# Attention's transposes and value products, taken for two groups of keys at a time

## The chip, the core and the metric

The kernel is one program on 1 core of one Trainium2 chip. The metric is the device time of one execution in microseconds (us). Three executions of the kernel before gave 2945.81, 2949.18 and 2950.16; their median is 2949.18.

## The reference, cut to what matters

One layer of a hybrid decoder on a sequence of 2048 tokens and 1024 channels, all in float32: a normalized input, one input projection, two kinds of causal attention with 8 heads of 64 channels each, an output projection, and a gated MLP with a short convolution. The change lies in the attention. Per head, with queries in blocks of 128:

```python
# forgetting attention ("fox")
s = jnp.einsum('bhqd,bhkd->bhqk', q_blk, k) * scale + F_blk[..., None] - F[:, :, None, :]
p = jax.nn.softmax(jnp.where(causal, s, -jnp.inf), axis=-1)
out = jnp.einsum('bhqk,bhkd->bhqd', p, v)
# stick-breaking attention ("sb")
log_one_minus_beta = jnp.where(strict, jax.nn.log_sigmoid(-z), 0.0)
rest = lax.cumsum(log_one_minus_beta, axis=3, reverse=True) - log_one_minus_beta
a = jnp.where(strict, jnp.exp(jax.nn.log_sigmoid(z) + rest), 0.0)
out = jnp.einsum('bhqk,bhkd->bhqd', a, v)
```

## The kernel before, in words

**Precision.** TensorE (PE) multiplies float32 operands in a rounded form (float32r). To keep accuracy an operand is stored as a high part (the rounded copy, made on ScalarE, ACT) and a low part (the value minus its high part, mostly made on VectorE, DVE), and a product becomes two or three matmuls.

**Order of the work.** Until about 1515 us the program runs 32 attention units: 4 head pairs times 4 blocks of 512 tokens, first of kind sb, then of kind fox. While `attend` goes through a unit, `interleave` steps other generators between its yields: the projections of later units (`proj`, lines 342 and 413 on PE), late conditioning work, and in the last two units the first output projection (line 912). The generators only give the order in which the program is traced. The framework's scheduler then sets the order on each engine, by its own estimate of when each instruction's inputs are ready. On the chip each engine takes its own queue in that order, and an instruction that waits holds up all behind it on its engine. `tc.issue_after(x)` puts what its block traces on the engine of `x` behind `x` in that engine's queue; it makes nothing wait for the end of `x`, and what the block traces on another engine is left as it is.

**A unit.** `attend` takes two pairs of query blocks and two heads. For each such head, `logits` (lines 596 and 597) multiplies queries by up to 512 keys into a PSUM bank of the tag qk (2 banks). In sb, ACT takes two sigmoids (630 and 631), GpSimd (POOL) masks (633), and DVE runs a scan from right to left (636) that leaves the weights of 128 queries in a tile `a`; keys are taken in chunks of 512 from the last to the first. In fox, DVE adds the forget sums (675) and ACT takes the exponential of the whole row (679), which leaves the weights in a tile `p`.

**A group.** `weighted` (600 to 618) takes 2 key tiles of 128 and 2 query blocks of 128: four transposes on PE (606) into a PSUM bank of the tag pt (3 banks), ordered (key 1, query 0), (key 0, query 0), (key 0, query 1), (key 1, query 1); on the diagonal the first of these is left out. ACT copies the bank to the high half of a tile `at` (610; `at` has 3 buffers), DVE writes the low half (611), and four value products (615) with `at` as the moving operand add to one PSUM bank `o` of the tag pv (1 bank; in the second-last unit the tag bc): per key tile first high, then low. A fox head with 2j + 2 key tiles has j + 1 groups, an sb chunk has one or two. After the head ACT and DVE read `o` (737, 738).

In all there are 576 groups with 2176 transposes and 2304 value products.

Of the kernel before, what the change touches and what calls it, by code (L numbers as in the profile page):

```python
# [12 lines left out]
AF = mybir.ActivationFunctionType  # L13
# [4 lines left out]
P = 128  # L18
# [16 lines left out]
def kernel(ctx: ExitStack, tc: tile.TileContext, x, c, w_ada, b_ada, g_attn, w_in, b_fgate,  # L35
                      g_out_fox, g_out_sb, w_out, g_mlp, w_up, conv_w, conv_b, w_down, g_final, out):
    nc = tc.nc
# [3 lines left out]
    def f(t):  # L41
        return t.bitcast(F32)
# [31 lines left out]
    ident = edge[:, TB - P:TB]  # L74
# [128 lines left out]
    last = {}  # L203
# [13 lines left out]
    b = pv()  # L217
# [6 lines left out]
    for r, src in ((R_GA, g_attn), (R_GM, g_mlp), (R_GF, g_out_fox), (R_GS, g_out_sb), (R_BA, b_ada)):  # L224
        n = src.shape[1] // P
# [368 lines left out]
    def logits(cw, qcols, hl, Q, K):  # L594
        b = qk()
        nc.tensor.matmul(b[:, :cw], Q[:, hl, 0, qcols], K[:, hl, :cw], start=True, stop=False)  # L596
        marks.append(nc.tensor.matmul(b[:, :cw], Q[:, hl, 1, qcols], K[:, hl, :cw], start=False, stop=True).ins)  # L597
        return b

    def weighted(o, kts, blk, V, hl, first, last, diag):  # L600
        b = pt()
        at = sb.tile([P, 2, 2 * 2 * P], F32R, name="at", tag="at", bufs=3)
        order = [(1, 0), (0, 0), (0, 1), (1, 1)]
        for i, (kk, qi) in enumerate(order):
            if not (diag and i == 0):
                nc.tensor.transpose(b[:, i * P:(i + 1) * P], blk(kts[kk], qi), ident)  # L606
        lo = P if diag else 0
        if diag:
            nc.scalar.activation(at[:, :, 0:P], edge[:, 0:2 * P].rearrange("p (a n) -> p a n", n=P), AF.Copy)
        copies = [nc.scalar.activation(at[:, 0, lo:], b[:, lo:], AF.Copy).ins,  # L610
                  nc.vector.tensor_sub(at[:, 1, lo:], b[:, lo:], f(at[:, 0, lo:])).ins]  # L611
        for kk, kt in enumerate(kts):
            for w in range(2):
                rhs = at[:, w].rearrange("p (s q) -> p s q", q=P)[:, 0:4:3, :] if kk else at[:, w, P:3 * P]
                m = nc.tensor.matmul(o[:, 0:2 * P], V[kt // 4][:, kt % 4, hl, :], rhs,  # L615
                                     start=first and kk == 0 and w == 0, stop=last and kk == 1 and w == 1)
        sums.append(m.ins)
        step[:] = [m.ins] + copies

    def sb_head(j, qc, hl, Q, K, V, o):  # L620
        n = (2 * j + 2 + 3) // 4
        right = [None, None]
        for ch in range(n - 1, -1, -1):
            at = []
            for qi in range(2):
                need = min(512, (2 * j + qi + 1) * P - ch * 512)
                b = logits(max(need, 2 * P), slice((qc + qi) * P, (qc + qi + 1) * P), hl, Q, K[ch])
                r = sx.tile([P, 512], F32, name="r", bufs=7)
                a = sx.tile([P, 512], F32, name="a", bufs=7)
                nc.scalar.activation(r[:, :need], b[:, :need], AF.Sigmoid)  # L630
                nc.scalar.activation(a[:, :need], b[:, :need], AF.Sigmoid, scale=-1.0)  # L631
                if right[qi] is None:
                    nc.gpsimd.affine_select(out=a[:, need - P:need], in_=a[:, need - P:need], pattern=[[-1, P]],
                                            base=-1, channel_multiplier=1, compare_op=ALU.is_ge, fill=0.0)
                rev = a[:, 0:need][:, ::-1]
                nc.vector.tensor_tensor_scan(rev, r[:, 0:need][:, ::-1], rev,  # L636
                                             0.0 if right[qi] is None else right[qi][:, 0:1], ALU.mult, ALU.add)
                right[qi] = a
                at.append(a)
            yield  # L640
            nk = min(4, 2 * j + 2 - 4 * ch)
            for m in range(0, nk, 2):
                kts = [4 * ch + m, 4 * ch + m + 1]
                weighted(o, kts, lambda kt, qi: at[qi][:, (kt - 4 * ch) * P:(kt - 4 * ch + 1) * P], V, hl,
                         ch == n - 1 and m == 0, ch == 0 and m == nk - 2, kts[0] == 2 * j)
                yield

    def load_sums(p):
        sums = [[], []]
# [7 lines left out]
    def fox_head(j, qc, hl, Q, K, V, o, Fb, ls):  # L657
        n = (2 * j + 2 + 3) // 4
        rows_ = []
        for qi in range(2):  # L660
            W = (2 * j + qi + 1) * P
            a = sx.tile([P, S], F32, name="p", bufs=4)
            mn = None
            for ch in range(n):
                need = min(512, W - ch * 512)
                b = logits(max(need, 2 * P), slice((qc + qi) * P, (qc + qi + 1) * P), hl, Q, K[ch])
                sl = slice(ch * 512, ch * 512 + need)
                m2 = sx.tile([P, 1], F32, name="mn", bufs=8)
                add = Fb[ch]
                if ch == n - 1:  # L670
                    add = px.tile([P, TB], F32, name="Fd", tag="hf_a", bufs=2)
                    mask[:] = [nc.gpsimd.affine_select(
                        out=add[:, :need], in_=Fb[ch][:, :need], pattern=[[-1, need]], base=need - P,
                        channel_multiplier=1, compare_op=ALU.is_ge, fill=BIG).ins]
                nc.vector.tensor_tensor_reduce(out=a[:, sl], in0=b[:, :need], in1=add[:, :need], scale=1.0,  # L675
                                               scalar=3e38 if mn is None else mn, op0=ALU.add, op1=ALU.min,
                                               accum_out=m2)
                mn = m2
            nc.scalar.activation(a[:, 0:W], a[:, 0:W], AF.Exp, scale=-1.0, bias=mn, accum_out=ls[:, hl, qc + qi:qc + qi + 1])  # L679
            rows_.append(a)  # L680
            yield
        for m in range(0, 2 * j + 2, 2):
            weighted(o, [m, m + 1], lambda kt, qi: rows_[qi][:, kt * P:(kt + 1) * P], V, hl, m == 0, m == 2 * j,
                     m == 2 * j)
            yield

    sums, step, mask = [], [], []
    deferred = []
# [137 lines left out]
    def attend_steps(u):  # L826
        kind, p, tb = u
        if kind == "fox":
            return sum(2 * (2 + 2 * tb + j2 + 1) for j2 in range(2)) + 1
        return sum(2 * (tb + 1 + 2 * tb + j2 + 1) for j2 in range(2)) + 1  # L830
# [199 lines left out]
    for i, u in enumerate(units):  # L1030
# [10 lines left out]
        n = attend_steps(u)  # L1041
# [212 lines left out]
    first = {"raw": [], "ws": []}  # L1254
# [41 lines left out]
    for u in range(1, NU):  # L1296
        for c in range(8 if u == 1 else 0, 16):
            t, n, q = chunk(u, c)
# [8 lines left out]
    def bank_a():  # L1307
        return bank(psd, "o", 4)
# [138 lines left out]
    for sblk, order in enumerate(orders):  # L1447
        after = None
        if sblk == 0:
# [5 lines left out]
            after = finish_last  # L1455
# [39 lines left out]
        a, b = bank_a(), bank_a()  # L1495
# [189 lines left out]
    for i in range(7):  # L1685
        nxt = {}
        kept = []
        for s in range(2):
# [4 lines left out]
            if left:  # L1693
                half, n = lefts[i]
                ops = left_over(s, half)
            for kp in range(NKP):
# [5 lines left out]
                w = bops[kp]  # L1702
# [60 lines left out]
```

## Time and profile before

| what | us |
| --- | --- |
| median of three executions | 2949.18 |
| lowest, highest | 2945.81, 2950.16 |
| span of the profiled execution, first to last instruction | 2941.4 |
| PE busy in it | 2867.8 |
| DVE, ACT, POOL busy | 2179.5, 1686.0, 901.1 |

The page gives the span alone for the profiled execution; the median of the timed ones is 7.8 us above that span, which is what lies around it. PE is an engine with two rows: PE is the matmul, PEld the load of the stationary operand, which goes beside the matmul before it. The trace models the end of a matmul, so its duration holds time in which the next one already streams; what a matmul costs is read from where a row of equal matmuls ends and the row after it ends.

### The profile page before, as it was taken

What the parts mean: (1) busy time and instruction counts of PE and PEld (TensorE: products, weight loads), DVE (VectorE), ACT (ScalarE), POOL (GpSimd) and SP (SyncE); (2) the same over time, 40 slices, a digit from 0 to 9 for tenths busy, and PEclk for the clock granted to TensorE, in tenths of its full rate; (3) what the DMA queues carried; (4) which work ended last, traced back from release to release, by engine and by line L of the source; (5) the groups of instructions that cost most, each with busy time, mean ns of one, the idle gap of its engine ahead of it and who ended that gap; (6) DMA issues with size and microseconds to landing.
All of it is one profiled execution on the core that took longest, in us unless ns stands there. A gap on an engine that the chain in (4) does not pass through costs nothing.

```text
span 2941.4 us, 45922 instructions
## 1 busy us (share of the span) xinstructions
PE 2867.8 (97%) x15772; PEld 2459.7 (84%) x15772; DVE 2179.5 (74%) x3464; ACT 1686.0 (57%) x3187; POOL 901.1 (31%) x967
## 2 busy tenths in 40 slices
PE   8999999999999999999999999999999999999998
PEld 7888888888988988888888788888788888888887
DVE  5787778877886656658843788888998888575476
ACT  5776767677776656658744554444444445433342
POOL 0431322243032423231213344444254543142200
PEclk8999999999999999999999999999999999999999
DMA  9749756867469794794537775554754444975644
GB/s 293 255 139 321 236 188 207 301 211 229 162 212 356 269 277 139 232 323 140 182 120 233 245 232 128 130 136 129 236 132 125 130 130 132 309 257 185 216 158 151
DMA packets 348346, 601.89 MB, mean 205 GB/s; under 512 B 34672, under 2 KB 178800, under 8 KB 348112
## 3 DMA queue, kind: packets, MB, share of 16 engines
q1 hardware_dynamic: 324208, 558.06, 57.7%
q0 software_dynamic: 10880, 20.97, 4.3%
q10 hardware_dynamic: 13024, 19.93, 1.9%
q8 instruction: 124, 2.03, 0.3%
q14 instruction: 110, 0.90, 0.1%
HBM read 420.77 MB, written 177.02 MB: 203 GB/s over the span
## 4 chain that ended last, share of the span: by engine, by line
PE 46%; DMA 3%; DVE 2%; SPq 1%; ACT 1%; issue 1%; POOL 0%; DVEq 0%; ACTq 0%; POOLq 0%
PE ps_o L1315 19%; PE ps_t L1315 7%; PE ps_o L1614 6%; PE ps_t L1614 3%; PE ps_bc L1614 3%; PE ps_o L912 1%; PE ps_pv L615 1%; DMA r<-rstd 1%; PE ps_bc L912 1%; PE ps_pt L606 1%; PE ps_o L1609 1%; DMA wo<-wos 1%; DMA hm<-hf_m 1%; SPq L895 1%; DVE op L46 1%
## 5 line engine op out<-in xcount | busy, mean ns | idle before, releaser
L1315 PE MATMUL ps_o<-op,wu 128*128 128x512 f32 x2592 | 608.0, 389 | 2.0 <-DVE snap L1366 1.5
L1315 PEld LDWEIGHTS ps_o<-op,wu 128*128 128x128 f32 x2592 | 486.2, 188 | 103.9 <-DVE snap L1366 1.9
L611 DVE TENSOR_TENSOR at<-ps_pt,at 128x512 fp32r<-128x512 f32 (+1 forms) x576 | 366.1, 652 | 100.2 <-ACT at L610 97.3
L636 DVE TENSOR_TENSOR_SCAN a<-r,a 128x512 f32<-128x512 f32 (+2 forms) x320 | 368.3, 1167 | 77.8 <-ACT a L631 39.9
L342 PE MATMUL ps_pj<-hp,w_qk 128*128 128x512 f32 x1512 | 411.2, 403 | 14.5 <-DMA hp<-hs 12.9
L610 ACT ACTIVATE at<-ps_pt 128x512 fp32r<-128x512 f32 (+1 forms) x576 | 318.5, 576 | 139.1 <-PE ps_pt L606 123.1
L615 PE MATMUL ps_pv<-at,V 128*128 128x256 f32 x2216 | 386.8, 292 | 9.3 <-DVE at L611 4.2
L615 PEld LDWEIGHTS ps_pv<-at,V 128*128 128x128 f32 x2216 | 320.9, 190 | 39.8 <-DVE at L611 11.4
L342 PEld LDWEIGHTS ps_pj<-hp,w_qk 128*128 128x128 f32 x1512 | 275.4, 190 | 71.0 <-DMA hp<-hs 16.2
L45 ACT ACTIVATE wu<-wuraw 128x512 fp32r<-128x512 f32 x204 | 128.9, 632 | 248.5 <-PE ps_o L1315 190.1
L596 PE MATMUL ps_qk<-K,Q 128*128 128x512 f32 (+2 forms) x640 | 265.7, 416 | 5.6 <-ACT a L631 3.3
L413 PE MATMUL ps_pj<-w_v,hp 128*128 128x256 f32 (+1 forms) x1536 | 236.6, 288 | 2.1 <-DVE hp L422 1.6
L597 PE MATMUL ps_qk<-K,Q 128*128 128x512 f32 (+2 forms) x640 | 235.7, 369 | 0.0
L1315 PE MATMUL ps_t<-op,wu 128*128 128x512 f32 x888 | 220.8, 390 | 1.0 <-DVE op L46 1.0
L413 PEld LDWEIGHTS ps_pj<-w_v,hp 128*128 128x128 f32 x1536 | 209.0, 189 | 10.9 <-DVE q L373 1.5
L630 ACT ACTIVATE r<-ps_qk 128x512 f32<-128x512 f32 (+2 forms) x320 | 173.1, 541 | 58.2 <-PE ps_qk L597 55.5
L46 DVE TENSOR_TENSOR wu<-wuraw,wu 128x512 fp32r<-128x512 f32 x204 | 189.6, 930 | 18.1 <-ACT wu L45 16.7
L1315 PEld LDWEIGHTS ps_t<-op,wu 128*128 128x128 f32 x888 | 166.4, 188 | 36.5 <-DVE op L46 1.8
L606 PE MATMUL ps_pt<-edge,a 128*128 128x128 f32 x1088 | 185.1, 274 | 8.4 <-DVE a L636 7.8
L1614 PE MATMUL ps_o<-op 128*128 128x512 f32 x840 | 191.5, 389 | 0.0
L1614 PEld LDWEIGHTS ps_o<-op 128*128 128x128 f32 x840 | 157.7, 188 | 32.7
L679 ACT ACTIVATE p<-p,mn 128x128 f32<-128x128 f32 (+15 forms) x128 | 153.9, 1203 | 53.3 <-DVE mn L675 52.2
(342 smaller groups left out, 5237.6 us busy)
## 6 DMA issues: line engine op xcount, KB each, us to landing
hp<-hs SPq DMA_DIRECT2D x224, 512.0 KB
wuraw<-in_w_up_dram SPq DMA_DIRECT2D x80, 512.0 KB
ra<-g SPq DMA_DIRECT2D x136, 256.0 KB
rb<-in_w_down_dram SPq DMA_DIRECT2D x108, 256.0 KB
g<-u SPq DMA_DIRECT2D x80, 256.0 KB
hs<-hp SPq DMA_DIRECT2D x32, 512.0 KB
hp<-in_w_ada_dram SPq DMA_DIRECT2D x32, 512.0 KB
qk_fox<-q SPq DMA_DIRECT2D x32, 512.0 KB
```

What stands on the lines that cost most here:

```text
L46: (lo_engine or nc.gpsimd).tensor_sub(lo, src, f(hi))
L342: nc.tensor.matmul(acc, w[kt][:, a, n], h[:, bb], start=kt == 0 and i == 0, stop=kt == KT - 1 and i == 2)
L413: nc.tensor.matmul(av[:, t * width:(t + 1) * width], hts[kt][:, a, tok], w[1][kt][:, bb, 0:width], start=kt == 0 and m == 0, stop=kt == KT ...
L596: nc.tensor.matmul(b[:, :cw], Q[:, hl, 0, qcols], K[:, hl, :cw], start=True, stop=False)
L597: marks.append(nc.tensor.matmul(b[:, :cw], Q[:, hl, 1, qcols], K[:, hl, :cw], start=False, stop=True).ins)
L606: nc.tensor.transpose(b[:, i * P:(i + 1) * P], blk(kts[kk], qi), ident)
L610: copies = [nc.scalar.activation(at[:, 0, lo:], b[:, lo:], AF.Copy).ins, nc.vector.tensor_sub(at[:, 1, lo:], b[:, lo:], f(at[:, 0, lo:])).ins]
L611: nc.vector.tensor_sub(at[:, 1, lo:], b[:, lo:], f(at[:, 0, lo:])).ins]
L615: m = nc.tensor.matmul(o[:, 0:2 * P], V[kt // 4][:, kt % 4, hl, :], rhs, start=first and kk == 0 and w == 0, stop=last and kk == 1 and w == 1)
L636: nc.vector.tensor_tensor_scan(rev, r[:, 0:need][:, ::-1], rev, 0.0 if right[qi] is None else right[qi][:, 0:1], ALU.mult, ALU.add)
L1315: nc.tensor.matmul(b, w[:, p, j], o[:, q], start=first and i == 0, stop=last and i == 2, skip_group_check=True)
L1614: nc.tensor.matmul(b, a[:, p, t * P:(t + 1) * P], w[:, q], start=first and i == 0, stop=last and i == 2, skip_group_check=True)
```

## The change

`weighted` is split into `turned` (transposes and copies of one group) and `summed` (its four products). The new `weighted` takes the groups of a chunk (sb) or of a head (fox) two by two:

- the transposes of both groups are traced first, then a yield, then the products of both groups, then a yield; an odd group goes alone, so that the number of yields stays as it was;
- within a group the transposes are traced in the reverse order, query 1 first, and all transposes of the pair stand behind its first one on PE;
- a product with the low part is now traced ahead of the one with the high part, and each product stands behind the one before it, across both groups;
- the first product of a pair is traced in an `issue_after` of the second group's low part, which is an instruction on DVE.

```diff
-    def weighted(o, kts, blk, V, hl, first, last, diag):
+    def turned(kts, blk, diag, lead):
         b = pt()
         at = sb.tile([P, 2, 2 * 2 * P], F32R, name="at", tag="at", bufs=3)
         order = [(1, 0), (0, 0), (0, 1), (1, 1)]
-        for i, (kk, qi) in enumerate(order):
+        for i in (3, 2, 1, 0):
+            kk, qi = order[i]
             if not (diag and i == 0):
-                nc.tensor.transpose(b[:, i * P:(i + 1) * P], blk(kts[kk], qi), ident)
+                with tc.issue_after(lead[0]) if lead else nullcontext():
+                    lead.append(nc.tensor.transpose(b[:, i * P:(i + 1) * P], blk(kts[kk], qi), ident).ins)
         lo = P if diag else 0
         if diag:
             nc.scalar.activation(at[:, :, 0:P], edge[:, 0:2 * P].rearrange("p (a n) -> p a n", n=P), AF.Copy)
-        copies = [nc.scalar.activation(at[:, 0, lo:], b[:, lo:], AF.Copy).ins,
-                  nc.vector.tensor_sub(at[:, 1, lo:], b[:, lo:], f(at[:, 0, lo:])).ins]
+        return kts, at, [nc.scalar.activation(at[:, 0, lo:], b[:, lo:], AF.Copy).ins,
+                         nc.vector.tensor_sub(at[:, 1, lo:], b[:, lo:], f(at[:, 0, lo:])).ins]
+
+    def summed(o, part, behind_, V, hl, first, last):
+        kts, at, copies = part
+        lead = behind_
         for kk, kt in enumerate(kts):
-            for w in range(2):
+            for w in (1, 0):
                 rhs = at[:, w].rearrange("p (s q) -> p s q", q=P)[:, 0:4:3, :] if kk else at[:, w, P:3 * P]
-                m = nc.tensor.matmul(o[:, 0:2 * P], V[kt // 4][:, kt % 4, hl, :], rhs,
-                                     start=first and kk == 0 and w == 0, stop=last and kk == 1 and w == 1)
+                with tc.issue_after(lead) if lead is not None else nullcontext():
+                    m = nc.tensor.matmul(o[:, 0:2 * P], V[kt // 4][:, kt % 4, hl, :], rhs,
+                                         start=first and kk == 0 and w == 1, stop=last and kk == 1 and w == 0)
+                lead = m.ins
         sums.append(m.ins)
         step[:] = [m.ins] + copies
+        return m.ins
+
+    def weighted(o, ms, blk, V, hl, first, end, diag):
+        for i in range(0, len(ms), 2):
+            lead = []
+            parts = [turned([m, m + 1], blk, m == diag, lead) for m in ms[i:i + 2]]
+            if len(parts) > 1:
+                yield
+            after = parts[-1][2][1] if len(parts) > 1 else None
+            for part in parts:
+                after = summed(o, part, after, V, hl, first and part[0][0] == ms[0], part[0][0] == end)
+            yield
```

What that makes of PE's queue is shown at two places. The names: ps_pt is the bank of a group's transposes, at its copies, ps_pv the head's sum, ps_qk logits, a and p the weights of one query block (sb and fox); L606 and L615 of before are L608 and L622 of the changed program. The first place is the middle of an sb head (the sum ps_pv_9331, at about 748 us of the trace); at_9415 is the first group of a chunk, and at_9427 of before and at_9423 of the changed program are the second. PE before:

```order
L615 MATMUL ps_pv_9331<-at_9415,V_8604 128x256
L606 MATMUL ps_pt_9466<-edge_249,a_9456 128x128 x2
L342 MATMUL ps_pj_9861<-hp_9862,w_qk_8381 128x512 x3
L615 MATMUL ps_pv_9331<-at_9415,V_8604 128x256 x3
L615 MATMUL ps_pv_9331<-at_9427,V_8604 128x256
L606 MATMUL ps_pt_9478<-edge_249,a_9448 128x128 x2
L606 MATMUL ps_pt_9478<-edge_249,a_9456 128x128 x2
L596 MATMUL ps_qk_9541<-K_8603,Q_8836 128x512
L597 MATMUL ps_qk_9541<-K_8603,Q_8836 128x512
L615 MATMUL ps_pv_9331<-at_9427,V_8604 128x256 x3
```

PE after the change, at the same groups:

```order
L342 MATMUL ps_pj_9861<-hp_9862,w_qk_8381 128x512 x3
L608 MATMUL ps_pt_9466<-edge_249,a_9456 128x128 x2
L608 MATMUL ps_pt_9466<-edge_249,a_9448 128x128 x2
L596 MATMUL ps_qk_9541<-K_8603,Q_8836 128x512
L597 MATMUL ps_qk_9541<-K_8603,Q_8836 128x512
L622 MATMUL ps_pv_9331<-at_9415,V_8604 128x256 x4
L608 MATMUL ps_pt_9474<-edge_249,a_9456 128x128 x2
L622 MATMUL ps_pv_9331<-at_9423,V_8604 128x256 x4
L608 MATMUL ps_pt_9474<-edge_249,a_9448 128x128 x2
```

The single first products, between which and the other three of their group other work stood, are gone. The transposes now begin with the query block whose weights come last (a_9456), and all four of ps_pt_9466 stand behind the projection's three matmuls. The pair's eight products are still parted by two transposes, and the eight transposes of the next pair (ps_pt_9466 and ps_pt_9474) by products and logits.

The second place is the start of the value products of the last fox head (the sum ps_pv_19424), where no logits are left and the output projection (ps_bc) is the only other work. PE before:

```order
L606 MATMUL ps_pt_19511<-edge_249,p_19425 128x128 x2
L606 MATMUL ps_pt_19511<-edge_249,p_19457 128x128 x2
L606 MATMUL ps_pt_19523<-edge_249,p_19425 128x128 x2
L606 MATMUL ps_pt_19523<-edge_249,p_19457 128x128 x2
L606 MATMUL ps_pt_19541<-edge_249,p_19425 128x128 x2
L606 MATMUL ps_pt_19541<-edge_249,p_19457 128x128 x2
L615 MATMUL ps_pv_19424<-at_19484,V_16955 128x256 x4
L912 MATMUL ps_bc_19504<-wo0_1_18372,mix_18341 128x512 x3
L912 MATMUL ps_bc_19504<-wo1_1_18373,mix_18341 128x512 x3
L912 MATMUL ps_bc_19642<-wo0_0_18364,mixq_18915 128x512 x3
L912 MATMUL ps_bc_19642<-wo1_0_18365,mixq_18915 128x512 x3
L615 MATMUL ps_pv_19424<-at_19512,V_16955 128x256 x4
```

PE after the change:

```order
L608 MATMUL ps_pt_19483<-edge_249,p_19457 128x128 x2
L608 MATMUL ps_pt_19483<-edge_249,p_19425 128x128 x2
L608 MATMUL ps_pt_19491<-edge_249,p_19457 128x128 x2
L608 MATMUL ps_pt_19491<-edge_249,p_19425 128x128 x2
L732 MATMUL ps_pt_19499<-headsel_257,sq_19228 128x2 x2
L622 MATMUL ps_pv_19424<-at_19484,V_16955 128x256 x4
L608 MATMUL ps_pt_19523<-edge_249,p_19457 128x128 x2
L608 MATMUL ps_pt_19523<-edge_249,p_19425 128x128 x2
L928 MATMUL ps_bc_19642<-wo0_0_18364,mixq_18915 128x512 x3
L928 MATMUL ps_bc_19642<-wo1_0_18365,mixq_18915 128x512 x3
```

The first group of the head (at_19484, from the bank ps_pt_19483) is now turned right ahead of its products, with one group's transposes and a small reduction between, where before three other groups' transposes and more stood between.

More of the change, by code (lines that the diff above doesn't have):

```diff
@@ L641, in sb_head @@
             nk = min(4, 2 * j + 2 - 4 * ch)
[L642 to L646, printed above, removed]
+            yield from weighted(o, range(4 * ch, 4 * ch + nk, 2),
+                                lambda kt, qi: at[qi][:, (kt - 4 * ch) * P:(kt - 4 * ch + 1) * P], V, hl,
+                                ch == n - 1, nk - 2 if ch == 0 else None, 2 * j)
     def load_sums(p):
@@ L681, in fox_head @@
             yield
[L682 to L685, printed above, removed]
+        yield from weighted(o, range(0, 2 * j + 2, 2), lambda kt, qi: rows_[qi][:, kt * P:(kt + 1) * P], V, hl,
+                            True, 2 * j, 2 * j)
     sums, step, mask = [], [], []
```

## The prediction

> **What bounds the kernel now.** I read the page's busy times first, then the busy time by stage, then the groups of instructions, and then what the transposes and value products waited for. The page says that PE does nearly all of the time:
>
> ```profile
> span 2941.4 us, 45922 instructions
> PE 2867.8 (97%) x15772; PEld 2459.7 (84%) x15772; DVE 2179.5 (74%) x3464; ACT 1686.0 (57%) x3187; POOL 901.1 (31%) x967
> ```
>
> By stage (length, then busy time of each engine, the granted clock, and the DMA share), the attention of kind sb, of kind fox, and the rest:
>
> ```profile
> core 0: us, PE busy (x) PEld busy (x) DVE busy (x) ACT busy (x) POOL busy (x), PEclk, DMA share, GB/s
> 130.00:870.00 740.00, 716.14 (x4734) 639.69 (x4732) 588.51 (x778) 541.30 (x1170) 194.76 (x244) 1.00 0.66 219
> 870.00:1515.00 645.00, 626.76 (x4107) 556.91 (x4106) 442.53 (x1137) 423.69 (x813) 184.77 (x260) 0.99 0.69 228
> 1515.00:2942.00 1427.00, 1408.73 (x6258) 1162.17 (x6258) 1059.29 (x1386) 638.94 (x1031) 486.32 (x428) 1.00 0.59 180
> ```
>
> The attention lasts 1385 us, and PE is idle for 23.9 + 18.2 = 42 us of it. ACT and DVE have slack on the whole. So an edit there can win or lose only through PE's work or through the waits in PE's queue. The groups concerned (count, busy time, mean ns, idle time ahead, who ended it):
>
> ```profile
> L615 PE MATMUL ps_pv<-at,V 128*128 128x256 f32 x2216 | 386.8, 292 | 9.3 <-DVE at L611 4.2 <-DVE oT L738 2.6 <-ACT at L610 1.6
> L606 PE MATMUL ps_pt<-edge,a 128*128 128x128 f32 x1088 | 185.1, 274 | 8.4 <-DVE a L636 7.8 <-DVE xm L567 0.2
> L606 PE MATMUL ps_pt<-edge,p 128*128 128x128 f32 x1088 | 168.2, 274 | 2.1 <-ACT p L679 1.1 <-DVE at L611 0.7
> L611 DVE TENSOR_TENSOR at<-ps_pt,at 128x512 fp32r<-128x512 f32 (+1 forms) x576 | 366.1, 652 | 100.2 <-ACT at L610 97.3
> L610 ACT ACTIVATE at<-ps_pt 128x512 fp32r<-128x512 f32 (+1 forms) x576 | 318.5, 576 | 139.1 <-PE ps_pt L606 123.1
> L342 PE MATMUL ps_pj<-hp,w_qk 128*128 128x512 f32 x1512 | 411.2, 403 | 14.5 <-DMA hp<-hs 12.9 <-POOL hp L46 1.3 <-ACT hp L45 0.3
> ```
>
> **PE's work: does regrouping save any?** The timeline of PE shows short and long runs of both kinds (start, duration, count):
>
> ```profile
> 1013.28 0.63 PE L615 MATMUL ps_pv<-at,V 128*128 128x256 f32 x4
> 1013.75 0.38 PE L606 MATMUL ps_pt<-edge,p 128*128 128x128 f32 x2
> 1013.89 0.60 PE L615 MATMUL ps_pv<-at,V 128*128 128x256 f32 x3
> 1014.33 0.38 PE L606 MATMUL ps_pt<-edge,p 128*128 128x128 f32 x2
> ...
> 1016.76 1.94 PE L413 MATMUL ps_pj<-w_v,hp 128*128 128x256 f32 x15
> 1018.54 0.82 PE L606 MATMUL ps_pt<-edge,p 128*128 128x128 f32 x6
> 1019.11 0.48 PE L596 MATMUL ps_qk<-K,Q 128*128 128x512 f32 x1
> ```
>
> Read by ends, start plus duration. The four products end at 1013.91, the two transposes at 1014.13, the three products at 1014.49, the next two transposes at 1014.71: 0.11 for a transpose in a run of two, 0.12 for a product right behind transposes. The 15 matmuls end at 1018.70 and the six transposes at 1019.36: again 0.11. The logits matmul behind them ends 0.23 later. So a change of kind costs nothing that two decimals show, 0 to 0.01 us. Counted through PE's whole queue, the transposes stand in 687 runs before and 484 after: 203 runs fewer, 0 to −2 us, and I take −0.5. The 2176 transposes (239 us) and 2304 products (276 us) themselves stay.
>
> The granted clock in those two stages is 1.00 and 0.99, with transposes in runs of up to twelve already at the second place shown above. Against longer runs speaks the Trainium skill, "TensorE: Matmul & The Clock Gate", Part 4: PE-mode transpose: in transpose mode the full clock is not engaged, since that work doesn't count as PE activity in the same way. By that rule more transposes in a row would pull the clock down; the 0.11 in runs of two and of six doesn't bear it out, but no row shows a queue made of longer runs, so it is kept as a rival below.
>
> **The waits.** What ended the idle time ahead of products and of transposes (us, times; the first three rows are those of the products):
>
> ```profile
>   DVE at L611: 20.3, 46
>   ACT at L610: 9.2, 17
>   DVE oT L738: 6.8, 10
> ```
>
> ```profile
>   DVE a L636: 17.4, 30
>   ACT p L679: 4.3, 8
> ```
>
> These lists add PE's idle time and that of its weight loads, so one wait can stand in them twice; I count half of what they say.
>
> *Products waiting for their operand.* Before, a product needs only ACT's copy for the high part, and the next one DVE's low part. The timeline of a late fox head shows the two steps:
>
> ```profile
> 1446.35 1.07 ACT L610 ACTIVATE at<-ps_pt 128x512 fp32r<-128x512 f32 x2
> 1446.98 0.39 PE L615 MATMUL ps_bc<-at,V 128*128 128x256 f32 x1 [0.45 <-ACT at L610]
> 1447.39 0.68 DVE L611 TENSOR_TENSOR at<-ps_pt,at 128x512 fp32r<-128x512 f32 x1
> 1448.12 0.74 PE L615 MATMUL ps_bc<-at,V 128*128 128x256 f32 x4 [0.52 <-DVE at L611]
> ```
>
> PE idles 0.45 for the copy, does one product, and idles 0.52 for the low part. With the low part first there is one wait instead, until the same 1448.12. The wait only gets shorter if the scheduler puts other work ahead of it. It does: the queue before has 183 runs of a single product, the changed one none. What a group needs when ACT and DVE are free is seen in the last unit:
>
> ```profile
> 1494.82 0.60 PE L606 MATMUL ps_pt<-edge,p 128*128 128x128 f32 x4
> 1495.46 0.60 ACT L610 ACTIVATE at<-ps_pt 128x512 fp32r<-128x512 f32 x1 [1.12 <-PE ps_pt L606]
> 1496.09 0.69 DVE L611 TENSOR_TENSOR at<-ps_pt,at 128x512 fp32r<-128x512 f32 x1 [1.16 <-ACT at L610]
> ```
>
> The transposes end at 1495.42 and the low part at 1496.78: 1.36 us, more when ACT or DVE are taken. I counted the PE work that stands between a group's last transpose and its first low product, with 0.11, 0.12 and 0.23 per matmul by the rows above. Under 2.0 us it is in 29 of 576 groups before and 40 after; under 3.0 us in 110 and 108. Of the tight ones 19 lie behind 1000 us of PE work, well in fox, before, and 34 after. In the last head shown above it is 0.44 for four transposes and 0.44 for the reduction (four short matmuls in the trace, at 0.11), so about 0.5 us of the 1.36 stays open. From half of 29.5 us: no change by the wider count, +5.6 (15 times 40/29 − 1) by the tighter one; I take +2, nearer to no change, because most groups have far more than 2 us. Ends: −5 (a third of these waits gone with the two-step waits) and +10 (first rival). Behind a waiting product stand logits and transposes on PE, so ACT's sigmoids and exponentials would be late by as much.
>
> *Transposes waiting for weights.* The scan comes last in an sb chain. The transposes now begin with query 1 and stand later: of 320 rows of sb weights, 38 have under 4 us of PE work between their logits and their first transpose before, 26 after; of 128 fox rows 30 and 28. A third of half of 17.4 is −3, fox nothing; ends −8 and +4. ACT's copies queue behind these transposes, but the bank pt is held for less time, as it is no longer filled in halves.
>
> *The sum's bank.* A head's first product waits until DVE has read the last head's sum (6.8 us, 10 times). Between the heads there are under 1.5 us of PE work in 11 of 131 places before and in 3 of 127 after. Three quarters of half of 6.8: −2.5; ends −3.4 and 0.
>
> *What only shifts.* The copies keep their engines and count. Loads on SP's queue change places too, with the release of their buffers; the projection's waits for them (12.9 us) could move by some 5 us either way, taken as 0.
>
> **Sum.** −0.5 + 2 − 3 − 2.5 = −4. Against the profiled execution's span that is 2937.4; with the 7.8 us between span and median, 2949.18 − 4 = 2945. About 0.2%, here 5.9 us, is what a measurement of this kernel can tell from no change, so this forecast lies inside that.
>
> **Rivals.** *Faster:* the single waits and the later transposes take away most of what they can, −8 for transposes, −5 for products, −2.5 for the bank: with the −0.5, 2933. For it: all two-step waits are gone, and three of the four counts improve. Against it: the tight groups in fox increase.
>
> *Slower:* the low part becomes the wait that counts in fox. The place is the first product of a pair in late fox units, where the next group's transposes and six output matmuls are all there is to fill 1.36 us. If each of the 34 tight groups there waits a whole low part of 0.65 us (L611's mean), that is 22 us against 12 for 19 before: +10, and if the gains elsewhere fail, 2959. It decides from about nine more such waits (9 × 0.65 = 5.9) that nothing pays for. For it speaks the last head shown above; against it the part ahead of that, whose tight groups fall from 10 to 6.
>
> *It doesn't do what it says:* the first product of a pair is put behind an instruction of DVE, and such an order binds only instructions of that engine; the queue shows eight transposes and eight products mostly parted by other work. Then little but the order within groups changes, and the waits come out even: 2949.
>
> *The clock:* if longer runs of transposes lower the granted clock from 1.00 and 0.99 by another 0.01 throughout the attention, 1385 us take 14 more: 2963. The Trainium skill's rule given with PE's work, that transposes don't count as activity, would work in this way.
>
> **How the numbers follow.** Forecast 0.40, of which 0.14 reaches past −5.9 (its own range is 2939 to 2951); faster rival 0.24; no effect 0.13; slower rival 0.19; the clock 0.04. Faster is 0.14 + 0.24 = 0.38, the same 0.26 + 0.13 = 0.39, slower 0.19 + 0.04 = 0.23. From 2931 to 2960 about 0.05 is left out below and 0.13 above (the clock, and the bad end of the slower rival), so the range holds 8 in 10.
>
> **What would show it.** Right: PE's busy time as before within a few us; waits of products for the ACT copy near nothing; waits for L613, the low part, up by a few us in fox; waits for the scan and for oT down. The first step falls if a transpose or a product costs another time than 0.11 or 0.12. The whole falls if waits of logits or of the projection's loads move by more than 6 us, if waits for the low part double, or if the granted clock of the attention changes.

## The result, and the profile after

The changed kernel takes 2963.11 us (median of six executions, 2955.91 to 2968.89) against 2948.89 for the kernel before (six, 2945.81 to 2953.7). The ratio is 1.0049, with a 95% interval of 1.0035 to 1.0063: 14 us slower, where 4 us less was forecast.

The page's busy times of the changed kernel, to be read against those of before:

```profile
span 2963.8 us, 45914 instructions
PE 2871.8 (97%) x15772; PEld 2463.1 (83%) x15772; DVE 2176.1 (73%) x3464; ACT 1684.7 (57%) x3188; POOL 901.1 (30%) x967
```

PE's busy time is 4 us longer, DVE and ACT are as they were. The stages of the changed kernel, with the ends of the attention's parts moved along:

```profile
130.00:875.00 745.00, 714.61 (x4732) 640.02 (x4731) 586.45 (x778) 539.39 (x1171) 196.76 (x246) 1.00 0.66 218
875.00:1532.00 657.00, 631.88 (x4130) 562.09 (x4129) 444.55 (x1140) 426.01 (x817) 184.55 (x260) 0.99 0.68 226
```

PE idles 30.4 + 25.1 = 56 us there, where it was 42. The granted clock of the two stages is the same, 1.00 and 0.99. The last value products, first of before and then of the changed kernel:

```profile
1513.84 0.53 PE L615 MATMUL ps_pv<-at,V 128*128 128x256 f32 x3
```

```profile
1530.81 0.63 PE L622 MATMUL ps_pv<-at,V 128*128 128x256 f32 x4
```

They end at 1514.4 and 1531.4. So 17 of the 22 us between the two profiled executions arise by the end of the attention. 5 more come behind it, in work that the change leaves in its order: there the changed kernel's trace has two stretches of 3.4 us at a granted clock of 0.50, at 1538 and 1664 us, which the trace of before has not; by estimate they cost half their length, 3.4 us together. (The two spans differ by 8 us more than the medians: the profiled execution of before was a short one.)

The groups of the changed kernel, for the rows shown of before:

```profile
L342 PE MATMUL ps_pj<-hp,w_qk 128*128 128x512 f32 x1512 | 404.1, 400 | 13.7 <-DMA hp<-hs 9.9 <-DVE hp L46 2.5 <-POOL hp L46 0.8
L613 DVE TENSOR_TENSOR at<-ps_pt,at 128x512 fp32r<-128x512 f32 (+1 forms) x576 | 365.5, 651 | 116.9 <-ACT at L612 114.5
L622 PE MATMUL ps_pv<-at,V 128*128 128x256 f32 x2216 | 358.1, 291 | 15.5 <-DVE at L613 12.1 <-DVE oT L754 3.3
L608 PE MATMUL ps_pt<-edge,a 128*128 128x128 f32 x1088 | 164.1, 273 | 12.6 <-DVE a L656 8.8 <-DVE at L613 2.4 <-ACT a L651 1.1
L608 PE MATMUL ps_pt<-edge,p 128*128 128x128 f32 x1088 | 156.5, 275 | 3.2 <-DVE at L613 1.5 <-ACT p L697 1.0 <-DVE var L738 0.4
```

A transpose and a product list the same mean duration as before (273 to 275 and 291 ns); less busy time per group only says that runs are longer and overlap inside a group. Idle time ahead of them is up from 9.3 to 15.5 for products and from 10.5 to 15.8 for transposes. What the products (first two rows) and then the transposes waited for:

```profile
  DVE at L613: 42.4, 63
  DVE oT L754: 8.1, 12
```

```profile
  DVE a L656: 14.8, 23
  DVE at L613: 9.4, 7
  ACT p L697: 4.7, 10
```

and the logits matmuls, which are in none of the prediction's terms, before and then after, first their row and then what they waited for:

```profile
L596 PE MATMUL ps_qk<-K,Q 128*128 128x512 f32 (+2 forms) x640 | 265.7, 416 | 5.6 <-ACT a L631 3.3 <-DVE mn L675 1.1 <-DMA K<-q 0.7
L596 PE MATMUL ps_qk<-K,Q 128*128 128x512 f32 (+2 forms) x640 | 257.7, 404 | 13.6 <-ACT a L651 8.3 <-DVE mn L693 2.3 <-DMA K<-q 1.9
```

```profile
  ACT a L631: 9.4, 17
  DVE mn L675: 6.4, 18
```

```profile
  ACT a L651: 21.7, 30
  DVE mn L693: 10.2, 26
```

A logits matmul needs a PSUM bank that ACT's sigmoids (sb) or DVE (fox) have read. Its waits doubled. With half of each list, as the prediction counted: products +6.5 (42.4 against 20.3 + 9.2), logits +8, transposes +2 (scan −1.3, low part +3.3, exponential +0.2), the bank +0.7. That is 17, the size of the loss by the end of the attention, but a match this close is luck: the lists are chosen, half of each is a rough rule, and waits that fell are left out. PE's own idle time rises by 13 us in the two stages and by 3 us ahead of 130 us (13.9 to 17.0). The transposes' wait for the low part had been no term of the prediction; before, their list had

```profile
  DVE at L611: 2.9, 7
```

### The profile page after: what moved, and what is told of

Same layout as the page of the kernel before. It is cut to its first block, busy times and chain, and to the rows that moved or that the text cites. A ratio compares the mean times of both kernels' runs of the same rounds, so it can differ in the third digit from the quotient of the medians.

```text
span 2963.8 us, 45914 instructions
## 1 busy us (share of the span) xinstructions
PE 2871.8 (97%) x15772; PEld 2463.1 (83%) x15772; DVE 2176.1 (73%) x3464; ACT 1684.7 (57%) x3188; POOL 901.1 (30%) x967
## 4 chain that ended last, share of the span: by engine, by line
PE 73%; DMA 14%; DVE 4%; ACT 3%; issue 2%; POOL 2%; SPq 1%; DVEq 0%; ACTq 0%; POOLq 0%
PE ps_o L1331 20%; PE ps_t L1331 7%; PE ps_pj L342 7%; PE ps_pv L622 6%; PE ps_o L1630 6%; PE ps_pt L608 5%; PE ps_pj L413 4%; PE ps_qk L596 3%; PE ps_t L1630 3%; PE ps_qk L597 3%; PE ps_bc L1630 3%; PE ps_o L928 2%; DMA hp<-hs 2%; DMA hp<-in_w_ada_dram 2%; PE ps_bc L928 1%
## 5 line engine op out<-in xcount | busy, mean ns | idle before, releaser
L342 PE MATMUL ps_pj<-hp,w_qk 128*128 128x512 f32 x1512 | 404.1, 400 | 13.7 <-DMA hp<-hs 9.9
L622 PE MATMUL ps_pv<-at,V 128*128 128x256 f32 x2216 | 358.1, 291 | 15.5 <-DVE at L613 12.1
L622 PEld LDWEIGHTS ps_pv<-at,V 128*128 128x128 f32 x2216 | 309.2, 190 | 41.8 <-DVE at L613 21.4
L596 PE MATMUL ps_qk<-K,Q 128*128 128x512 f32 (+2 forms) x640 | 257.7, 404 | 13.6 <-ACT a L651 8.3
L597 PE MATMUL ps_qk<-K,Q 128*128 128x512 f32 (+2 forms) x640 | 235.4, 369 | 0.0
L413 PE MATMUL ps_pj<-w_v,hp 128*128 128x256 f32 (+1 forms) x1536 | 223.9, 286 | 1.5 <-DVE hp L422 1.3
L46 DVE TENSOR_TENSOR op<-ra,op 128x512 fp32r<-128x512 f32 x144 | 105.5, 740 | 99.1 <-ACT op L45 98.7
```

The costliest lines, as they stand in the source:

```text
L46: (lo_engine or nc.gpsimd).tensor_sub(lo, src, f(hi))
L342: nc.tensor.matmul(acc, w[kt][:, a, n], h[:, bb], start=kt == 0 and i == 0, stop=kt == KT - 1 and i == 2)
L413: nc.tensor.matmul(av[:, t * width:(t + 1) * width], hts[kt][:, a, tok], w[1][kt][:, bb, 0:width], start=kt == 0 and m == 0, stop=kt == KT ...
```

## The experiments

The first theory behind the loss was that *pairs* cost it: eight copies and products in one go keep ACT and PE from the logits. Its first rival was that the *parts* inside a group do it (low part first, transposes reversed). The second was that neither does, and that any new order of the queues moves the waits; this split later into a form without a sign (*reshuffle*) and one with a sign (*lost fit*: the order of before happens to suit the chip well, and nearly any other is slower). Each run below was timed against the kernel before on the same chip.

### The parts, one by one

**Groups alone** (the changed kernel, without pairs):

```diff
-        for i in range(0, len(ms), 2):
+        for i in range(0, len(ms)):
...
-            parts = [turned([m, m + 1], blk, m == diag, lead) for m in ms[i:i + 2]]
+            parts = [turned([m, m + 1], blk, m == diag, lead) for m in ms[i:i + 1]]
```

> The changed kernel with each group alone: reversed transposes, low part first and the chained products stay, the pairing goes. Pairing theory (two groups' copies and products in one go hold up the logits behind them): the loss goes, 2949 +- 3, and waits of logits for a bank fall back from about 27 to 17 us. Parts theory (the order inside a group makes the loss): still 2957 to 2965. Reshuffle theory (any new order of the queues moves the waits by some 10 us either way): anywhere from 2940 to 2965, with no relation to which part is kept.

Measured: 2962.77, ratio 1.0050 (1.0033 to 1.0066). The loss stays though the pairs are gone, and the logits still wait as in the changed kernel (19.8 us for ACT and 14.4 for DVE in their list, against 21.7 and 10.2): the pairing theory falls.

**High part first** (the changed kernel, with pairs):

```diff
-            for w in (1, 0):
+            for w in range(2):
...
-                                         start=first and kk == 0 and w == 1, stop=last and kk == 1 and w == 0)
+                                         start=first and kk == 0 and w == 0, stop=last and kk == 1 and w == 1)
```

> The changed kernel with the high part's product ahead of the low part's again; pairs and reversed transposes stay. Pairing theory: no change against the changed kernel, 2963 +- 4. Parts theory, low part first as the cause: 2952 or less, and the products' wait for the low part falls by 6 us. Reshuffle theory: anywhere from 2940 to 2970.

Measured: 2970.35, ratio 1.0070 (1.0051 to 1.0088). The two-step waits are back and the products wait longer than in the changed kernel:

```profile
L622 PE MATMUL ps_pv<-at,V 128*128 128x256 f32 x2216 | 390.7, 293 | 19.5 <-ACT at L612 10.2 <-DVE at L613 5.2 <-DVE oT L754 3.8
```

So low part first is no loss within pairs. With it the products idle for 15.5 us instead of 19.5; the two ratios, 1.0049 and 1.0070, overlap in their intervals.

**Low part first alone** (the kernel before, group by group):

```diff
-            for w in range(2):
+            for w in (1, 0):
...
-                                     start=first and kk == 0 and w == 0, stop=last and kk == 1 and w == 1)
+                                     start=first and kk == 0 and w == 1, stop=last and kk == 1 and w == 0)
```

> The kernel before with only the low part's product put ahead of the high part's, group by group. Pairing theory: 2949 +- 3. Parts theory, low part first as the cause: 2955 to 2960, with the products' waits up by 6 us. Reshuffle theory: anywhere from 2940 to 2965.

Measured: 2958.83, ratio 1.0038 (1.0026 to 1.0051). Products waited 35.0 us for the low part and no longer for the copy (before 20.3 and 9.2); half of the difference is 3 us of the 11:

```profile
  DVE at L611: 35.0, 54
  DVE oT L738: 3.7, 6
```

**Reversed transposes alone** (the kernel before):

```diff
-        for i, (kk, qi) in enumerate(order):
+        lead = []
+        for i in (3, 2, 1, 0):
+            kk, qi = order[i]
             if not (diag and i == 0):
-                nc.tensor.transpose(b[:, i * P:(i + 1) * P], blk(kts[kk], qi), ident)
+                with tc.issue_after(lead[0]) if lead else nullcontext():
+                    lead.append(nc.tensor.transpose(b[:, i * P:(i + 1) * P], blk(kts[kk], qi), ident).ins)
```

> The kernel before with only the four transposes of a group reversed and put behind the first of them. Pairing theory: 2949 +- 3. Parts theory, the transposes as the cause (copies come later on ACT, and sigmoids behind them free the logits' banks later): 2955 to 2960, with waits of logits up by 8 us. Reshuffle theory: anywhere from 2940 to 2965.

Measured: 2962.71, ratio 1.0041 (1.0027 to 1.0056). The expected place, logits that wait for sigmoids, hardly moved (3.3 to 3.7 us for ACT). Idle time ahead of products went from 9.3 to 13.6 us and ahead of transposes from 10.5 to 15.7, and the mean granted clock was 0.988 in this trace against 0.993 before:

```profile
L618 PE MATMUL ps_pv<-at,V 128*128 128x256 f32 x2216 | 388.1, 293 | 13.6 <-ACT at L613 5.0 <-DVE at L614 4.7 <-DVE oT L741 3.4
L596 PE MATMUL ps_qk<-K,Q 128*128 128x512 f32 (+2 forms) x640 | 257.2, 403 | 6.8 <-ACT a L634 3.7 <-DVE mn L678 2.6
```

Each part costs 11 to 14 us by itself, both together cost the same 14, and each through other waits. That is not how parts with a price of their own add up, and it called for a control.

### Controls: numbers that have nothing to do with groups

All four are the kernel before with one edit, in this order: projections held back by 11 logits; reductions a step earlier; due times at 0.79; the two middle transposes in each other's place.

```diff
-    LAG, ENDQ = 12, 16
+    LAG, ENDQ = 11, 16
...
-            deferred.append([reduce, 13])
+            deferred.append([reduce, 12])
...
-            yield max(first + (due - first) * min(1.0, m / (0.8 * n)),
+            yield max(first + (due - first) * min(1.0, m / (0.79 * n)),
...
-        for i, (kk, qi) in enumerate(order):
+        for i in (0, 2, 1, 3):
+            kk, qi = order[i]
```

> The kernel before with one number changed that has nothing to do with groups: projections are held back by 11 logits instead of 12. The scheduler then deals a new order to PE, DVE and ACT. Parts theory (low part first and reversed transposes cost time as such, 11 and 12 us alone): 2949 +- 5. Lost-fit theory (the order before is one that happens to fit, and any other deal waits more): 2955 to 2965, with waits up by 8 to 18 us on all kinds of matmuls. Reshuffle theory without a sign: anywhere from 2938 to 2962.

> The kernel before with the small reductions behind a pair of heads put one step earlier (12 instead of 13). Parts theory: 2949 +- 5. Lost-fit theory: 2955 to 2965. Reshuffle theory without a sign: anywhere from 2938 to 2962.

> The kernel before with the projections' due times at 0.79 of a unit instead of 0.80. Parts theory: 2949 +- 5. Lost-fit theory: 2955 to 2965. Reshuffle theory without a sign: anywhere from 2938 to 2962.

> The kernel before with the second and third transpose of each group traced in each other's place, so that the two of key 1, query 0 and key 0, query 1 come first; low and high parts as before. Parts theory with the reversal as a cause: half of it at most, 2949 to 2955. Lost-fit theory: 2955 to 2965. Reshuffle theory without a sign: anywhere from 2938 to 2962.

Measured:

| run | us | ratio (95%) |
| --- | --- | --- |
| lag 11 | 2964.39 | 1.0052 (1.0034 to 1.0069) |
| reductions 12 | 2976.57 | 1.0093 (1.0077 to 1.0110) |
| pace 0.79 | 2969.70 | 1.0077 (1.0063 to 1.0092) |
| middle swapped | 2972.61 | 1.0080 (1.0066 to 1.0093) |

The kernel before took 2947.08 on that chip, so all four are slower, by 17 to 29 us, with no change to what a group does or nearly none. The parts theory needed 2949 for the first three. All four lie above the range of the theory without a sign. Lost fit had the sign right in all four, and its size too small in three (expected up to 2965).

The traces say where the controls lost their time, and it is not waits alone. From 130 us to the last value product of each trace (us; half clock is the time with a granted clock of 0.50):

| kernel | last value product ends | PE idle | at half clock |
| --- | --- | --- | --- |
| before | 1514.4 | 42.0 | 17.1 |
| the change | 1531.4 | 55.5 | 17.1 |
| lag 11 | 1527.0 | 43.7 | 37.5 |
| reductions 12 | 1539.8 | 54.9 | 44.4 |
| pace 0.79 | 1538.1 | 52.0 | 37.5 |
| middle swapped | 1540.5 | 55.3 | 44.4 |

In all five the later end is, within 4 us, the added idle time plus half of the added time at half clock. The waits that lost fit expected for lag 11, up by 8 to 18 us, did not come: PE idles 1.7 us more there, and the clock accounts for the rest. In the other three idle time rises by 10 to 13 us, as in the change, and the clock takes about as much again; the change loses nothing to the clock in its attention.

### Twins: the change on other orders

If before is one order that fits, the change has to be weighed on others. The same numbers were set in the changed kernel (the first three edits above). A fourth run was meant to make the change's words true on PE, by putting a pair's first product behind the pair's last transpose:

```diff
-            after = parts[-1][2][1] if len(parts) > 1 else None
+            after = lead[-1] if len(parts) > 1 else None
```

> The changed kernel with projections held back by 11 logits, as in the run of that name on the kernel before (2964, ratio 1.0052). Lost-fit theory (the change loses the good deal of before and by itself is worth about what was forecast, -4 to -8): a ratio of 1.002 to 1.004 to the kernel before, some 5 us under its twin. If the change itself costs 14 us: a ratio of about 1.010, 2978. If nothing but chance rules: no relation to the twin.

> The changed kernel with the reductions one step earlier; its twin on the kernel before took 2977, ratio 1.0093. Lost-fit theory: a ratio of 1.005 to 1.008. If the change itself costs 14 us: 1.014, 2990. If nothing but chance rules: 1.003 to 1.010.

> The changed kernel with due times at 0.79 of a unit; its twin on the kernel before took 2970, ratio 1.0077. Lost-fit theory: a ratio of 1.004 to 1.007. If the change itself costs 14 us: 1.0125, 2984. If nothing but chance rules: 1.003 to 1.010.

> The changed kernel with a pair's first product really put behind the pair's last transpose on PE (in the change it stands behind an instruction of DVE, which binds nothing there). Lost-fit theory: one more deal, 2958 to 2975. If batching as such saves or costs: under 2955, with products' waits for the low part down by 10 us, or over 2980 with them up by 15.

Measured, each twin as a ratio to the kernel before:

| edit | without the change | with the change | difference |
| --- | --- | --- | --- |
| none | 1 | 1.0049 | +0.0049 |
| lag 11 | 1.0052 | 1.0092 (1.0074 to 1.0110) | +0.0040 |
| reductions 12 | 1.0093 | 1.0047 (1.0030 to 1.0065) | −0.0046 |
| pace 0.79 | 1.0077 | 1.0061 (1.0042 to 1.0080) | −0.0016 |

In us these are 2977.58, 2963.25 and 2967.37. Of the three twins pace 0.79 came out as expected of lost fit, though its two ratios overlap in their intervals; reductions 12 came out a little better than expected; and lag 11 went the other way, near the 1.010 of a change that costs 14 us by itself. Their mean difference is −0.0007, 2 us, with 12 us of scatter to either side. So a fixed price of 14 us for the change itself does not hold in two of the three, and a gain of its own of 4 to 8 us is not shown either.

These orders are fewer than the rows of the table. Place by place, by tiles and shapes, the list of PE's 15772 matmuls in the trace of the changed kernel with pace 0.79 differs from the changed kernel's at 582 places, where the changed kernel differs from the one before at 5126: this twin is the change nearly over again.

The fourth run took 2960.73, ratio 1.0041 (1.0025 to 1.0056), but it is no new order at all. In PE's queue of the changed kernel the first product of each of the 256 pairs already stands behind the pair's last transpose, so the edit moves nothing: the traces of the two list the same instructions in the same order on every engine. The run is the change measured again on another chip, and it agrees with the first measurement (1.0049). Whether real batching, with a pair's eight transposes and its eight products each in one go, would gain or lose is not tested.

### Confined edits: the place, or the order behind it

Next the edits were confined to some units. Units without pairs use the old `weighted`; with no unit chosen, PE's queue is that of before, place by place.

```diff
+        paired[0] = (kind, p) == ("sb", 0)
...
+        paired[0] = (kind, p) == ("fox", 3)
...
-            deferred.append([reduce, 13])
+            deferred.append([reduce, 12 if (kind, p) == ("sb", 0) else 13])
...
-            deferred.append([reduce, 13])
+            deferred.append([reduce, 12 if (kind, p) == ("fox", 3) else 13])
```

> Pairs in the first four units only (40 of 576 groups). PE's queue differs from before at 744 places of 15553, all among the first 1800, and is the same behind. Lost-fit theory: the loss follows the share of the queue that is dealt anew, 744 of the 5014 places that the full change moves: +2, 2949 to 2953. If the edit costs by its own groups: +1.

> Pairs in the last four fox units only. PE's queue differs at 488 places, all behind 8450. The traces of the two kernels put 10 of their 17 us in the attention behind 1300 us, so if that loss belongs to these places: +6 to +10, 2955 to 2959. Lost-fit theory by share: +1.5, 2949 to 2953.

> The kernel before with the reductions one step earlier in the first four units only. It moves 4176 places of PE's queue, from 624 to 8214, though the edit itself touches four units. Lost-fit theory: most of the loss of the full edit (2977) comes, +12 to +25. If an edit costs only where it is made: 2949 to 2953.

> The kernel before with the reductions one step earlier in the last four fox units only: 507 places of PE's queue differ, nearly all behind 8500. Lost-fit theory by share: +1 to +4. If the end of the attention is the place that counts: +6 to +10.

and, with the same switch, `kind == "sb" and p > 0` and `kind == "fox" and p < 3`:

> Pairs in the twelve sb units of head pairs 2 to 4 only; 2905 places of PE's queue differ, from 1730 to 7174, so some fox units are dealt anew as well. Lost-fit theory by share (2905 of 5014 places): +8. If pairs cost by their kind and sb is harmless, as its tight groups suggested: within 4 us of before.

> Pairs in the fox units of head pairs 1 to 3 only; 1946 places of PE's queue differ, from 5282 to 8534. Lost-fit theory by share: +5. If the pairs cost in fox, where the low part is the tight wait: +10 to +14.

Measured, with the number of places of PE's queue (15553 in all) at which it differs from before:

| run | places | us | ratio (95%) |
| --- | --- | --- | --- |
| pairs, first four units | 744 | 2952.22 | 1.0004 (0.9990 to 1.0018) |
| pairs, other sb units | 2905 | 2959.85 | 1.0032 (1.0020 to 1.0045) |
| pairs, first 12 fox units | 1946 | 2952.51 | 1.0007 (0.9995 to 1.0019) |
| pairs, last four units | 488 | 2949.80 | 0.9997 (0.9985 to 1.0008) |
| pairs everywhere (the change) | 5014 | 2963.11 | 1.0049 (1.0035 to 1.0063) |
| reductions, first four units | 4176 | 2968.28 | 1.0064 (1.0043 to 1.0086) |
| reductions, last four units | 507 | 2956.47 | 1.0016 (1.0005 to 1.0027) |
| reductions everywhere | 4354 | 2976.57 | 1.0093 (1.0077 to 1.0110) |

The third run of the four is the clearest. It moves a handful of reductions (two matmuls each) in the first four units by one step and nothing else in the program's text, yet the scheduler deals 4176 places anew, through the sb and most of the fox units, and it costs 18 us. It deals nearly the order of pace 0.79: PE's lists in the two traces differ at 406 of the 15772 places, counted as for the twins. The pairs in the same four units change every group there, but PE's queue falls back into the old order at once, and the cost is within 0.2%. So the loss follows what is dealt anew behind an edit more than the edit. It is no price per place, though: by share the pairs in the first 12 fox units should have cost 5 us, and they cost 2 with an interval that includes none; in the last units the reductions cost 5 us with 507 places, and the pairs none with 488.

Within the pairs, most of the loss comes with those in the sb units behind the first four, and with the fox units that these deal anew. There logits waited for the sigmoids as they do in the full change, with pairs in these units alone:

```profile
L596 PE MATMUL ps_qk<-K,Q 128*128 128x512 f32 (+2 forms) x640 | 262.8, 412 | 14.3 <-ACT a L678 8.0 <-DVE mn L720 4.8 <-DMA K<-q 0.6
```

The full change has 13.6 in that row's place. The run with the reductions moved loses its time elsewhere; its logits wait less than those of before, 4.5 against 5.6, and its products wait for the head's bank:

```profile
L596 PE MATMUL ps_qk<-K,Q 128*128 128x512 f32 (+2 forms) x640 | 264.3, 414 | 4.5 <-ACT a L631 3.1 <-DVE mn L675 1.0
L615 PE MATMUL ps_pv<-at,V 128*128 128x256 f32 x2216 | 390.3, 292 | 19.9 <-DVE oT L738 10.1 <-DVE at L611 5.4 <-ACT at L610 3.0
```

Two orders that both lose (9 and 18 us), with different waits: no one wait is the cause.

## Why the prediction was wrong, point by point

**PE's work: right.** 0.11 and 0.12 us per transpose and product hold; listed durations are the same, and PE's busy time moved by 4 us of 2868. Fewer runs (484 for 687) brought nothing that shows.

**The 7.8 us around the span: wrong, without effect on the forecast.** The profiled execution of the changed kernel took 2965.51 with a span of 2963.8, so 1.7 us lie around a span. If the same 1.7 lay around that of before, its profiled execution was some 6 us under its median; the sum was a difference to the median, and so untouched.

**Products waiting for their operand: the direction right, too small.** Forecast +2 with +5.6 by the tighter count; measured +6.5 by the same halves. The tight count, groups with under 2 us of other work, was the better one.

**Transposes: wrong.** −3 was forecast from more work ahead of them. The wait for the scan fell by 1.3, but the wait for a PSUM bank of the tag pt, held until the low part is taken, rose by 3.3. The prediction had said that this bank is held for less time.

**The sum's bank: wrong.** −2.5 forecast, +0.7 measured, although more work stands between the heads.

**What only shifts: the step that failed.** "Taken as 0" were the waits that the change doesn't touch by name. Of these the projection's wait for its loads did stay (9.9 against 12.9). The logits were not in the list at all, and they gave +8, the largest term (15.8 us in their list before, 31.9 after). The prediction's words for them, that they stand behind a waiting product, give the way it happens in this queue; no size was put to it. Two of the signs by which the whole was to fall came: waits of logits that move by more than 6 us, and products' waits for the low part that double (20.3 to 42.4).

Behind this lies a wider fault, and the controls show it. The sum priced an edit at its own groups, and set all else at "comes out even". But an edit deals a new order to thousands of places in the queues, and against the order of before that does not come out even: twelve of twelve different kernels whose attention was dealt anew throughout, the changed one among them, took 1.0038 to 1.0093 of its time. The third rival, that little but the order changes, was near in that and wrong in its price of 2949; on this kernel the price of "only another order" is 10 to 29 us. Its ground was only half right: the order that binds DVE alone does bind nothing on PE, but PE's queue has the first product of every pair behind the pair's last transpose all the same.

**The slower rival: right in sign and near in time (2959), wrong in place.** It put the loss into fox, in late units with thin cover. The pairs in the last four units cost nothing, and those in the other fox units 2 us with an interval that includes none. The pairs in the sb units behind the first four, for which the tight groups spoke well, bring 9 us.

**The clock: not it.** 1.00 and 0.99 in both, with a mean of 0.992 over the span against 0.993, and 17.1 us at half clock in the attention of both. That the rival's number, 2963, is the measured time is luck.

What stays open is why the order of before fits so well. The runs show that it lies under all the others tried, not by which property. One plain reading, that numbers such as 12, 13 and 0.80 had been picked by timing this kernel, so that nearly any neighbour is slower, no run here tests. Nor do they part, inside the sb units, the cost of the pairs from that of the order which they bring: the share of the places moved would give +8, and +9.4 was measured, but the other confined runs show that the loss is no steady price per place.

## What to carry to other kernels

Where a scheduler deals the queues and one engine is 97% busy, time an unrelated small edit before an effect below 1% is put down to a change: here an order of no meaning cost 17 to 29 us, and the change 14. A change is better weighed on several orders, each with its twin, or confined so that the rest of the queue stays as it was; and a forecast for such a kernel needs a term for the order that is lost, which is not centred on zero when the kernel before is the best order at hand.

## What the runs showed of the hardware that was not expected

**Half the clock behind a wait.** Late in the changed kernel's fox part PE was busy for 3.45 of 5 us, and then had a granted clock of 0.50 for 10 us. The windows (PE's busy time is the second number, the granted clock the third from the end):

```profile
1405.00:1410.00 5.00, 4.39 (x33) 3.77 (x32) 4.73 (x14) 4.91 (x10) 0.90 (x2) 1.00 0.02 3
1410.00:1415.00 5.00, 3.45 (x22) 2.47 (x20) 2.56 (x6) 4.46 (x8) 0.99 (x2) 1.00 0.50 112
1415.00:1420.00 5.00, 5.00 (x24) 4.80 (x23) 2.96 (x10) 1.51 (x4) 0.02 (x1) 0.51 1.00 217
1420.00:1425.00 5.00, 5.00 (x24) 4.81 (x23) 2.12 (x7) 2.70 (x5) 0.29 (x1) 0.50 1.01 356
```

and PE's timeline at its start, where a transpose waits 1.49 us for a bank, and in the slow stretch, where eight transposes take 1.91 us instead of 1.04:

```profile
1409.89 1.04 PE L608 MATMUL ps_pt<-edge,p 128*128 128x128 f32 x8
...
1413.36 0.55 PE L608 MATMUL ps_pt<-edge,p 128*128 128x128 f32 x3 [1.49 <-DVE at L613]
...
1423.48 1.91 PE L608 MATMUL ps_pt<-edge,p 128*128 128x128 f32 x8
```

At half speed such a stretch costs up to 5 us. It is no part of the change's loss: the trace of before has as much time at half clock in its attention, at 167, 1051 and 1208 us. A busy row hides it: PE reads 5.00 of 5.

The Trainium skill, "TensorE: Matmul & The Clock Gate", Part 4: PE-mode transpose, has transposes not count as activity for that gate in the usual way. The stretch agrees with this as far as it goes, with eight and three transposes ahead of it. The traces taken together speak for PE's idle time instead. In the 20 traces 120 stretches at 0.50 begin between 130 and 1540 us, of 3.4, 6.8 or 10.2 us; in 111 of them PE had idled for more than 1 us of the 3.4 us ahead, and in 45 no transpose stood in these 3.4 us. Of the windows of that length which no such stretch follows, under 3% hold as much idle time. How much is enough stays open: the kernel before had PE busy for only 3.66 us in 1400 to 1405 and kept a clock of 1.00. Its window, in the same columns:

```profile
1400.00:1405.00 5.00, 3.66 (x27) 3.00 (x26) 3.89 (x11) 4.04 (x9) 1.02 (x2) 1.00 0.85 211
```

**The clock goes with the spread of one kernel.** Of 19 executions of the kernel before on one chip, the shortest took 2943.20 us at a mean granted clock of 0.993 and the longest 2960.10 at 0.987; 0.006 of 2943 is 17.7 us, and the two differ by 16.9. Between them the order is looser: another execution at 0.993 took 2950.46. The four controls had means of 0.9875 to 0.9887 over their executions, where the kernel before had 0.9915 on that chip: 0.003 to 0.004, or 8 to 12 us, of their 17 to 29 us goes with the clock. Since the stretches begin behind idle time, that is in the main a result of PE's waits. On the chip of the twins the four kernels had 0.9893 to 0.9917 and the kernel before 0.9899, so there the clock accounts for 2 us of loss at most.
